# A two-layer diffusion trunk on one core: loading its beginning by single feature tiles, and its last MLP by token tile

## The chip, the cores and the metric

The kernel runs on one core of a Trainium2 chip. The core's engines run beside each other and wait for each other by semaphores: TensorE (PE for its matmuls, PEld for the loads of their stationary operand), VectorE (DVE), ScalarE (ACT), GpSimd (POOL), and SyncE (SP), from whose queue all of this kernel's transfers are issued. Each engine takes its instructions in a fixed order. The metric is the device time of one execution in microseconds (us), lower being better.

## The reference

Two layers over 256 latent tokens and 256 context tokens, model width 1024, all in float32. Cut to what matters here:

```python
for l in range(DEPTH):                                   # DEPTH = 2
    sh1, sc1, g1, sh2, sc2, g2 = ada_mod(c[:, None, :], w_ada[l], b_ada[l])
    u = x * (1.0 + sc1) + sh1                            # the same for the context
    p = split_proj(u @ w_in[l] + b_in[l])                # 76 tiles of 128 columns
    y_a, y_b = local_branches(p, ...)                    # short gated conv | Conformer conv
    y_c = diff_post(diff_latent(q_d, k_d, v_d, ...))     # differential attention
    y_d = na_latent(q_n, k_n, v_n, ...)                  # neighbourhood attention
    y = merge_out(p[I_GATE], (y_a, y_b, y_c, y_d), w_branch[l], b_branch[l], w_o[l])
    x = layer_norm(DEEPNORM_ALPHA * x + g1 * y, ln_g[l, 0], ln_b[l, 0])
    x = layer_norm(DEEPNORM_ALPHA * x + g2 * sq_relu_ffn(x * (1.0 + sc2) + sh2, w_ff1[l], w_ff2[l]),
                   ln_g[l, 1], ln_b[l, 1])
```

`ada_mod` multiplies silu(c) by `w_ada` and gives shifts, scales and gates. In the last layer the context gives only keys and values, so that layer's MLP works on 256 tokens.

## The kernel before, in words

Every product is made of three matmuls: an operand is split into a rounded part and its remainder (for a weight `whi` and `wlo`, for an activation the two tiles of `u`), and `mm3` sums whi x u_hi, whi x u_lo and wlo x u_hi. Weights come in units of 128x1024: a transfer into `raw`, ScalarE makes `whi`, VectorE `wlo`. Units of which both parts are put into two tiles of 512 columns each are called `wh` and `wl`. Activations stand transposed: eight feature tiles k of 128 features, with the 512 tokens (256 latent, 256 context) as columns. A projection unit is eight feature tiles times three matmuls.

Nothing is ordered by hand. Each part of the work is a Python generator with a priority, and `Sched.run` is a list scheduler that has costs of its own for each operation and emits the earliest operation, then the one with the smaller priority number. The order of each engine's instructions comes out of that, and it is fixed in the program.

**The beginning.** The first layer's first modulation (shift and scale) is a product with 8 MB of `w_ada`. `ada_first` does it in four steps j; a step loads eight tiles `a0` (one per 128 rows of the sum, 256 KB each) that give two feature tiles' shift and scale. `ada_first_step` sums them in PSUM (`ada`), copies them (`adrow`), transposes them (`adT`), adds the bias and gives `mod` and `G`. `first_x` loads the input by pairs of feature tiles, latent and context apart (`x0`); `to_u` makes `u` of them. `w_load` puts the first five units' transfers between these (`W_AFTER`), and `first_unit` runs those five products (matrices `M_CA`, `M_CG` of the convolution), each waiting for the pairs of `u`.

**The last layer's MLP input.** `out_proj` multiplies by `w_o` (`wo`), and `residual` and `norm_tile` normalise two token tiles of 128 (tile 0 and tile 1) into `r`. Then `to_u` transposes both tiles by pairs of feature tiles (`uT`), applies scale and shift (`uf`) and splits into `u`. `ff1_rows` runs the first three MLP units k by k over all 256 columns. `LO_AFTER` holds back the remainder `wlo` of the second of these units until tile 1 is normalised.

**The end.** The last product is run for tile 0 and then for tile 1, in two halves of 256 columns. `residual` adds, `norm_tile` waits for the statistics, `normalise` gets 1/sqrt of the variance from GpSimd and applies it with two `stt` (scalar_tensor_tensor) per half row, and `store_out` writes each half.

Of the kernel before, what the change touches and what calls it, by code (L numbers as in the profile page):

```python
# [12 lines left out]
ALU = mybir.AluOpType  # L13
# [12 lines left out]
FIRST = 5  # L26
# [287 lines left out]
class Kernel(Sched):  # L314
# [207 lines left out]
    def constants(self):  # L522
        nc = self.nc
        self.cT = self.const([128, 16], "cTs")
# [31 lines left out]
    def silu_c(self):  # L556
        th = self.const([128, 16], "cth")
        yield self.act(th, self.cT, AF.Tanh, scale=0.5)
        yield self.ts(th, th, 0.5, 0.5, ALU.mult, ALU.add)
        yield self.tt(self.cs[:, :, 0:2], self.cT.re("p (k s) -> p k s", s=2), th.re("p (k s) -> p k s", s=2), ALU.mult)  # L560
        self.signal("cs")
# [5 lines left out]
    def layer_constants(self, l):  # L567
# [3 lines left out]
        if l:  # L571
            yield self.dma(sm, self.SM[l], 128 * NSM * 4)
        else:
            yield self.wait("raw", FIRST - 1)
            yield self.dma(self.rope, self.rope_t.rearrange("c p t -> p c t"), 1 << 18)
# [21 lines left out]
    def w_load(self):  # L597
        for i, (l, name) in enumerate(self.order):
            if i < FIRST:
                yield self.wait("x0", 1, W_AFTER[i])  # L600
# [4 lines left out]
    def w_hi(self):  # L605
        for i in range(len(self.order)):
            yield "prio", 3 if i >= FIRST else FIRST_PRIO
# [5 lines left out]
            else:  # L613
                hi = yield self.alloc("wt", "whi", dt=F32R, name="whi", n=1)
                yield self.act(hi[0], raw, AF.Copy)
            self.signal("whi", i, val=(raw, hi))

    def w_lo(self):
        for i in range(len(self.order)):
            yield "prio", 3 if i >= FIRST else FIRST_PRIO  # L620
# [7 lines left out]
            else:  # L628
                lo = yield self.alloc("wt", "wlo", dt=F32R, name="wlo", n=1)
                yield self.tt(lo[0], raw, hi[0].f, ALU.subtract)  # L630
# [19 lines left out]

    def weight_order(self):
        o = []
        for l in range(DEPTH):
            a = lambda *n: o.append((l, n))
            for ct in range(4):
                a("in", M_CA + ct)
                a("in", M_CG + ct)
# [123 lines left out]
    def ada_first(self):  # L781

        modv = self.modT[0].ap[:, 0:16, :].rearrange("p (c k) s -> p c k s", c=2)
        G = self.const([128, 8, 2], "G00")
        self.aff[0, 0] = G, self.modT[0][:, 0:8, :]
        for j in range(4):
            if j:
                yield self.wait("raw", max(i for i, a in enumerate(W_AFTER) if a < j))
            raws = []
            for k in range(KD):  # L790
                raw = yield self.s("", F32, "a0")
                yield self.dma(raw, self.w_ada0[j, k], 1 << 18)
                raws.append(raw)
            if j == 0:
                yield self.dma(self.sm[0], self.SM[0], 128 * NSM * 4)
            self.signal("a0", j)
            self.spawn(self.ada_first_step(j, raws, modv, G), 6)

    def ada_first_step(self, j, raws, modv, G):
        nc = self.nc  # L800
        yield self.wait("cs")
        ps = yield self.alloc("ps", "ada", name="ada0")
        step = CHUNK if j else 1
        for k0 in range(0, KD, step):
            calls = [(ps.ap[32 * q:32 * q + 32, 0:128], self.cs.ap[:, k, :], raws[k].ap[:, q * 128:q * 128 + 128], k == 0,
                      k == KD - 1, {"tile_position": (0, 32 * q)}) for k in range(k0, k0 + step) for q in range(4)]
            yield self.mm(calls, [ps], [*raws[k0:k0 + step], self.cs], 290 * step)
            self.release(*raws[k0:k0 + step])
# [5 lines left out]
        src = t.ap[:, 0:128].rearrange("p (c k r) -> p c k r", c=2, k=2)[:, :, :, 0:2]  # L814
        out = modv[:, :, 2 * j:2 * j + 2, :]
        b = self.sm[0][:, _SM["ada"]:_SM["ada"] + 16].ap.rearrange("p (c k) -> p c k", c=2)[:, :, 2 * j:2 * j + 2]
        b = b.unsqueeze(3).to_broadcast([128, 2, 2, 2])
        yield self.dve(80, lambda: nc.vector.tensor_tensor(out=out, in0=src, in1=b, op=ALU.add), [self.modT[0]],
                       [t, self.sm[0]])
        self.release(t, row)  # L820
        g = G[:, 2 * j:2 * j + 2, :]
        yield self.ts(g, self.modT[0][:, 8 + 2 * j:10 + 2 * j, :], 1.0, None, ALU.add)
        self.signal("aff", 0, 0, j)
# [52 lines left out]
    def ucut(self, l, j, k, a, b):  # L876

        out = []
        for v in self.u[l, j][k]:
            bufs = v.bufs if a < 256 < b else (v.bufs[0],) if b <= 256 else (v.bufs[1],)  # L880
            out.append(V(v.ap[:, a:b], bufs))
        return out

# [4 lines left out]
    def to_u(self, l, j, s, tiles):  # L888

        yield self.wait("newu", l, j)
        for kp in range(4):
            yield self.wait("aff", l, j, kp)
            G, B = self.aff[l, j]
            if tiles is None:
                t = yield self.wait("x0", s, kp)
            else:
                t = yield self.alloc("ps", "att", name="uT")
                outs, ins = [], []
                for kk in range(2):  # L900
                    for i in range(2):
                        k = 2 * kp + kk
                        o = kk * 256 + i * 128
                        outs.append(t[:, o:o + 128])
                        ins.append(tiles[i][k // 4][:, (k % 4) * 128:(k % 4) * 128 + 128])
                yield self.transposes(outs, ins)
# [14 lines left out]
    def first_x(self):  # L921
        for s in range(2):
            self.spawn(self.to_u(0, 0, s, None), 7)
        for kp in range(4):
            yield self.wait("a0", kp)
            for s in range(2):
                t = yield self.s("", F32, "x0")
                yield self.dma(t, self.x_t[s, kp], 1 << 18)
                self.signal("x0", s, kp, val=t)

    def first_proj(self, ms, n):

        ps = []
        for i, m in enumerate(ms):
            assert self.order[i] == (0, ("in", m))
            self.spawn(self.first_unit(i, n), 40)
        for i, m in enumerate(ms):
            p = yield self.wait("first", i)
            ps.append(p)
        self.w_next = len(ms)  # L940
        self.signal("pace", 0)
# [12 lines left out]

    def first_unit(self, i, n):
        w = yield self.wait("w", i)
        w = Weight(w, 128)
        p = yield self.alloc("ps", "first", name="mm")
        for k in range(KD):
            for s in range(2):  # L960
                yield self.wait("uk", 0, 0, s, k // 2)
            a, b = w(k), self.ucut(0, 0, k, 0, n)
            yield self.mm(self.mm3(p[:, 0:n], a, b, k == 0, k == KD - 1), [p], [*a, *b], 3 * (0.4167 * n + MM))
        self.release(*w.views())
        self.signal("first", i, val=p)
# [485 lines left out]
    def normalise(self, r, stv, ns, gb=None):  # L1451
# [77 lines left out]
    def after_attn_norm(self, l, s, rs):  # L1529

        for i in range(2):
            yield self.wait("z", l, 0, 2 * s + i)
        self.spawn(self.make_x1(l, s, rs), PRIO_X)
# [386 lines left out]
```

## Time and profile before

| | |
|---|---|
| median of 3 runs | 1597.26 us (1596.98 to 1599.57) |
| profiled execution | 1597.91 us, span 1596.0 us |
| TensorE matmuls busy | 1560.8 us (98%), 8688 matmuls |
| weight loads busy | 1336.3 us (84%) |
| VectorE busy | 1306.3 us (82%) |
| ScalarE busy | 870.5 us (55%) |
| read from memory | 250.67 MB |
| mean granted TensorE clock | 0.994 |

The span goes from the first to the last instruction of the profiled execution; its own time has 1.9 us around that. Rows of a profile's timeline are start, length, engine, line, operation, output<-inputs and shape, xN for N instructions in a row; in brackets stands how long the engine had been idle and what ended it. Lengths of pipelined matmuls overlap: the distance of two starts is the rate, the length of one is its latency. Everything of the kernel's helpers is recorded at a few lines (L434 for matmuls, L387, L394 and L414 for VectorE), so tiles tell what a row is.

### The profile page before, as it was taken

What the parts mean: (1) busy time and instruction counts of PE and PEld (TensorE: products, weight loads), DVE (VectorE), ACT (ScalarE), POOL (GpSimd) and SP (SyncE); (2) the same over time, 40 slices, a digit from 0 to 9 for tenths busy, and PEclk for the clock granted to TensorE, in tenths of its full rate; (3) what the DMA queues carried; (4) which work ended last, traced back from release to release, by engine and by line L of the source; (5) the groups of instructions that cost most, each with busy time, mean ns of one, the idle gap of its engine ahead of it and who ended that gap; (6) DMA issues with size and microseconds to landing.
All of it is one profiled execution on the core that took longest, in us unless ns stands there. A gap on an engine that the chain in (4) does not pass through costs nothing.

```text
span 1596.0 us, 23002 instructions
## 1 busy us (share of the span) xinstructions
PE 1560.8 (98%) x8688; PEld 1336.3 (84%) x8688; DVE 1306.3 (82%) x2206; ACT 870.5 (55%) x1411; POOL 12.4 (1%) x51
## 2 busy tenths in 40 slices
PE   6999999999999999999999999999999999989997
PEld 4878888888888788888787878989997999989997
DVE  3999999499999746987687796999999796765566
ACT  3465367454755544742423334766576786476553
POOL 0000000000000000000000000000000000000000
PEclk9999999999999999999999999999999999999999
DMA  9322221455455155456555654533443445645563
GB/s 356 128 73 80 94 91 67 149 181 175 149 176 181 50 171 188 139 186 197 170 192 186 229 185 149 194 127 130 148 140 119 146 158 172 238 146 185 198 223 107
DMA packets 80707, 254.30 MB, mean 159 GB/s; under 512 B 9028, under 2 KB 13892, under 8 KB 80596
## 3 DMA queue, kind: packets, MB, share of 16 engines
q1 hardware_dynamic: 80596, 252.84, 46.7%
q8 instruction: 68, 1.11, 0.3%
q14 instruction: 43, 0.35, 0.1%
HBM read 250.67 MB, written 2.13 MB: 158 GB/s over the span
## 4 chain that ended last, share of the span: by engine, by line
PE 58%; DVE 8%; ACT 1%; issue 1%; POOLq 0%; POOL 0%; DVEq 0%; ACTq 0%
PE mm L434 29%; PE f L434 16%; PE wo L434 4%; PE br L434 4%; DVE wlo L387 2%; DVE conf L414 1%; PE nv L434 1%; PE o L434 1%; PE dv L434 1%; PE PT L494 1%; DVE qk L387 1%; DVE st L1194 1%; PE S L434 0%; DVE pt L387 0%; PE uT L494 0%
## 5 line engine op out<-in xcount | busy, mean ns | idle before, releaser
L434 PE MATMUL mm<-u,whi 128*128 128x512 f32 (+1 forms) x3168 | 786.2, 339 | 0.8 <-ACT u L380 0.3
L434 PEld LDWEIGHTS mm<-u,whi 128*128 128x128 f32 x3168 | 544.8, 190 | 67.9 <-issue 2.8
L434 PE MATMUL mm<-u,wlo 128*128 128x512 f32 (+1 forms) x1584 | 534.1, 337 | 0.6 <-DVE wlo L387 0.6
L387 DVE TENSOR_TENSOR wlo<-raw,whi 128x1024 fp32r<-128x1024 f32 x335 | 408.3, 1220 | 146.7 <-PE mm L434 62.3
L380 ACT ACTIVATE whi<-raw 128x1024 fp32r<-128x1024 f32 x335 | 353.9, 1057 | 320.0 <-DVE wlo L387 115.8
L434 PEld LDWEIGHTS mm<-u,wlo 128*128 128x128 f32 x1584 | 301.1, 190 | 32.6 <-DVE wlo L387 0.8
L434 PE MATMUL f<-whi,a 128*128 128x512 f32 (+1 forms) x760 | 235.3, 388 | 0.0
L414 DVE SCALAR_TENSOR_TENSOR sums<-araw,cs,sums 128x512 f32<-128x512 f32 x280 | 195.2, 745 | 12.5 <-DMA araw<-in_w_ada 12.1
L434 PEld LDWEIGHTS f<-whi,a 128*128 128x128 f32 x760 | 142.3, 188 | 29.7 <-issue 0.8
L434 PE MATMUL f<-wlo,a 128*128 128x512 f32 (+1 forms) x380 | 147.1, 387 | 0.0
L414 DVE SCALAR_TENSOR_TENSOR conf<-glu,sm,conf 128x512 f32<-128x512 f32 (+1 forms) x240 | 137.4, 613 | 0.7
L434 PEld LDWEIGHTS f<-wlo,a 128*128 128x128 f32 x380 | 71.4, 188 | 14.2
L380 ACT ACTIVATE P<-S,st 128x512 f32<-128x512 f32 (+1 forms) x96 | 58.7, 614 | 31.1 <-DVE st L1194 30.7
L434 PE MATMUL wo<-whi,mg 128*128 128x512 f32 (+1 forms) x184 | 56.6, 382 | 0.0
L380 ACT ACTIVATE gth<-mm,hb 128x512 f32<-128x512 f32 (+1 forms) x64 | 36.8, 574 | 34.7 <-PE mm L434 34.5
L1194 DVE TENSOR_REDUCE st<-S 128x1 f32<-128x512 f32 (+1 forms) x96 | 55.1, 589 | 0.3
L434 PE MATMUL S<-qk 128*128 128x512 f32 (+1 forms) x192 | 48.5, 367 | 3.7 <-ACT qk L380 1.2
L380 ACT ACTIVATE qk<-ra 64x512 fp32r<-64x512 f32 (+1 forms) x67 | 37.7, 563 | 22.7 <-DVE ra L387 21.4
L380 ACT ACTIVATE bh<-br,hb 128x512 f32<-128x512 f32 (+1 forms) x64 | 36.3, 573 | 20.8 <-PE br L434 20.6
L380 ACT ACTIVATE a2f<-mm 128x512 f32<-128x512 f32 (+1 forms) x64 | 30.7, 481 | 30.5 <-PE mm L434 30.5
L387 DVE TENSOR_TENSOR a<-a2f,a 128x512 fp32r<-128x512 f32 (+1 forms) x64 | 35.4, 554 | 11.4 <-ACT a L380 11.4
L434 PE MATMUL dv<-whi,u 128*128 128x512 f32 x128 | 43.3, 398 | 0.5 <-ACT P L380 0.5
(206 smaller groups left out, 1907.2 us busy)
## 6 DMA issues: line engine op xcount, KB each, us to landing
raw<-in_W SPq DMA_DIRECT2D x344, 512.0 KB
araw<-in_w_ada SPq DMA_DIRECT2D x80, 512.0 KB
a<-in_w_ada SPq DMA_DIRECT2D x32, 256.0 KB
bt<-in_rpb SPq DMA_DIRECT2D x32, 128.0 KB
row<-g SPq DMA_DIRECT2D x12, 256.0 KB
x<-in_x_t SPq DMA_DIRECT2D x8, 256.0 KB
row<-in_ln_g SPq DMA_DIRECT2D x8, 256.0 KB
row<-in_ln_b SPq DMA_DIRECT2D x8, 256.0 KB
```

Of the source, the lines that this page charges most:

```text
L380: lambda: nc.scalar.activation(out=out.ap, in_=in_.ap, func=func, **kw),
L387: return self._op(eng, cost, lambda: e.tensor_tensor(out=out.ap, in0=x.ap, in1=y.ap, op=op), [out], [x, y])
L414: return self._op("DVE", cost, lambda: nc.vector.scalar_tensor_tensor(out=out.ap, in0=x.ap, scalar=a(s), in1=y.ap, op0=op0, op1=op1), [out ...
L434: nc.tensor.matmul(out=out, lhsT=x, rhs=y, start=start, stop=stop, **kw)
L494: nc.tensor.transpose(o.ap, i.ap, ident.ap)
L1194: yield self.dve(68 + 1.04 * nk, lambda: nc.vector.tensor_reduce(out=mx.ap, in_=S.ap, axis=AX.X, op=ALU.max, negate=True), [mx], [S])
```

## The change

It has four parts.

1. The beginning goes by single feature tiles. `load_all` issues for each k four modulation tiles (each now two of the eight rows of the sum, for one feature tile's shift and scale), the input's tile (latent and context together), and one transfer `W0[k]` with the k-th rows of six units (128x768). `ada_first` is run for each k; its sums of even and odd rows stand apart and are added after the transpose. `first_u` makes `u` of one k, 512 columns wide, and `first_proj` runs six units' products for that k into six PSUM banks. The biases of the modulation come with `cT`.
2. In the last layer `to_u_tile` makes the MLP's input for one token tile as soon as that tile is normalised, and `ff1_rows` runs tile 0's products for all k (128 columns each) and then tile 1's. The first MLP unit is among those that are kept in tiles of 512 columns.
3. In the last normalisation tile 0's `norm_tile` gets priority 40 instead of 1.
4. `normalise` emits the first `stt` of both halves ahead of the second ones.

```diff
+    def load_all(self):
+        for k in range(KD):
+            raws = []
+            for i in range(4):
+                raw = yield self.s("", F32, "a0")
+                yield self.dma(raw, self.w_ada0[k, i], 1 << 18)
+                raws.append(raw)
+            self.spawn(self.ada_first(k, raws), 6)
+            t = yield self.s("", F32, "x0")
+            yield self.dma(t, self.x_t[k], 1 << 18)
+            self.signal("x0", k, val=t)
+            raw = yield self.alloc("wt", "raw", name="raw")
+            yield self.dma(raw[:, 0:FIRST * 128], self.W0[k], FIRST * 128 * 512)
+            self.signal("raw", k, val=raw)
...
     def ada_first(self, j, raws):
         yield self.wait("cs")
         ps = yield self.alloc("ps", "ada", name="ada0")
+        for i, raw in enumerate(raws):
+            yield self.mm([(ps.ap[32 * q:32 * q + 32, 0:128], self.cs.ap[:, 2 * i + q // 2, :],
+                            raw.ap[:, q * 128:q * 128 + 128], i == 0, i == 3, {"tile_position": (0, 32 * q)})
+                           for q in range(4)], [ps], [raw, self.cs], 290)
+            self.release(raw)
...
     def first_proj(self, ms, n):
+        for m in ms:
+            p = yield self.alloc("ps", "first", name="mm")
+            ps.append(p)
+        for k in range(KD):
+            hi, lo = yield self.wait("w", k)
+            yield self.wait("u0", k)
+            b = self.ucut(0, 0, k, 0, n)
+            for i, p in enumerate(ps):
+                a = hi[0][:, i * 128:i * 128 + 128], lo[0][:, i * 128:i * 128 + 128]
+                yield self.mm(self.mm3(p[:, 0:n], a, b, k == 0, k == KD - 1), [p], [*a, *b], 3 * (0.4167 * n + MM))
...
+    def to_u_tile(self, l, j, i, tile):
+        yield self.wait("newu", l, j)
+        for h in range(2):
+            t = yield self.alloc("ps", "att", name="uT")
+            yield self.transposes([t[:, q * 128:q * 128 + 128] for q in range(4)],
+                                  [tile[h][:, q * 128:q * 128 + 128] for q in range(4)])
+            f = yield self.s("tmp", F32, "uf")
+            for q in range(4):
+                k = 4 * h + q
...
+                c = slice(q * 128, q * 128 + 128)
+                yield self.affine_any(f[:, c], t[:, c], G[:, k, 0:1], B[:, k, 0:1])
+                yield from self.split(f[:, c], *self.ucut(l, j, k, i * 128, i * 128 + 128))
+                self.signal("uk", l, j, i, k)
...
     def normalise(self, r, stv, ns, gb=None):
             for c, h in enumerate(r):
                 yield self.stt(h, h, mv[:, 0:1], g[c], ALU.subtract, ALU.mult)
+            for c, h in enumerate(r):
                 yield self.stt(h, h, rs, b[c], ALU.mult, ALU.add)
                 self.signal("out", c, h.bufs[0])
...
     def after_attn_norm(self, l, s, rs):
+        if self.by_tile(l, 1):
+            for i in range(2):
+                yield self.wait("z", l, 0, i)
+                self.spawn(self.to_u_tile(l, 1, i, rs[i]), 2)
...
     def ff1_rows(self, l, ms, n):
-        for k in range(KD):
-            yield self.wait("uk", l, 1, 0, k // 2)
-            for p, w in zip(ps, ws):
-                a, b = w(k), self.ucut(l, 1, k, 0, n)
-                yield self.mm(self.mm3(p[:, 0:n], a, b, k == 0, k == KD - 1), [p], [*a, *b], 3 * (0.4167 * n + MM))
+        for i in range(n // 128):
+            for k in range(KD):
+                yield self.wait("uk", l, 1, i, k)
+                for p, w in zip(ps, ws):
+                    a, b = w(k), self.ucut(l, 1, k, i * 128, i * 128 + 128)
+                    yield self.mm(self.mm3(p[:, i * 128:i * 128 + 128], a, b, k == 0, k == KD - 1), [p], [*a, *b],
+                                  3 * (0.4167 * 128 + MM))
...
-                self.spawn(self.norm_tile(l, 1, t, yacc[t], sts[t]), 1)
+                self.spawn(self.norm_tile(l, 1, t, yacc[t], sts[t]), 40 if l == DEPTH - 1 and t == 0 else 1)
...
-                          if l == DEPTH - 1 and (n[:2] == ("wo", 1) and n[2] < 2 or n[:3] == ("f2", 3, 1) and n[3] < 2)}
+                          if l == DEPTH - 1 and (n == ("f1", 0) or n[:2] == ("wo", 1) and n[2] < 2 or n[:3] == ("f2", 3, 1) and n[3] < 2)}
```

Three places show what this does to the order. The first is TensorE (PE) in the beginning, where products (`mm`) and sums of the modulation (`ada`, one row for a tile `a`) follow each other. Before:

```order
L434 MATMUL mm<-u,wl 128x512
L434 MATMUL ada_328<-a_218,cs 32x128 x4
L434 MATMUL ada_328<-a_220,cs 32x128 x4
L434 MATMUL ada_328<-a_222,cs 32x128 x4
L434 MATMUL ada_328<-a_229,cs 32x128 x4
L434 MATMUL mm<-u,wh 128x512 x2
L434 MATMUL mm<-u,wl 128x512
L434 MATMUL mm<-u,wh 128x512 x2
```

And now, at a similar place (the fifth feature tile's modulation among the third's and fourth's products):

```order
L431 MATMUL mm<-u,wlo 128x512
L431 MATMUL ada_379<-a_221,cs 32x128 x4
L431 MATMUL mm<-u,whi 128x512 x2
L431 MATMUL mm<-u,wlo 128x512
L431 MATMUL ada_379<-a_223,cs 32x128 x4
L431 MATMUL mm<-u,whi 128x512 x2
L431 MATMUL mm<-u,wlo 128x512
L431 MATMUL ada_379<-a_225,cs 32x128 x4
L431 MATMUL mm<-u,whi 128x512 x2
L431 MATMUL mm<-u,wlo 128x512
L431 MATMUL ada_379<-a_227,cs 32x128 x4
```

Four tiles that stood together stand singly between products: behind the first product there are 19 such switches for 26 tiles, where there were five for 24.

The second place is the last layer's MLP input. On PE, from the last `wo` of tile 1; each feature tile's transpose is one `uT`. Before:

```order
L434 MATMUL wo<-whi,mg 128x256
L494 MATMUL uT<-ident,r 128x128 x8
L434 MATMUL mm<-u,whi 128x256 x2
L434 MATMUL mm<-u,wlo 128x256
L434 MATMUL mm<-u,whi 128x256 x2
```

And now, where the twelve transposes are tile 0's eight and the first four of tile 1:

```order
L431 MATMUL wo<-whi,mg 128x256
L491 MATMUL uT<-ident,r 128x128 x12
L431 MATMUL mm<-u,wh 128x128 x2
L431 MATMUL mm<-u,wl 128x128
L431 MATMUL mm<-u,whi 128x128 x2
L431 MATMUL mm<-u,wlo 128x128
```

The products have half the columns and twice the number, and tile 1's first transposes stand ahead of all of them. On VectorE (DVE) at the same place, from tile 1's last residual (`r<-wo`) to the two remainders `wlo` that wait for tile 1's normalisation (`r<-r,st`). Before:

```order
L387 TENSOR_TENSOR r<-wo,row 128x256
L414 SCALAR_TENSOR_TENSOR r<-x_13348,r 128x256
L1492 BN_STATS st<-r 128x6
L1456 BN_AGGR st<-st 128x2
L394 TENSOR_SCALAR st<-st 128x1 x2
L394 TENSOR_SCALAR r<-r,st 128x512
L387 TENSOR_TENSOR wlo<-raw,whi 128x1024 x2
```

And now:

```order
L384 TENSOR_TENSOR r<-wo,row 128x256
L391 TENSOR_SCALAR uf<-uT,G_13581,B_13582 128x128
L411 SCALAR_TENSOR_TENSOR r<-x_13352,r 128x256
L1524 BN_STATS st<-r 128x6
L384 TENSOR_TENSOR u<-uf,u 128x128
L1487 BN_AGGR st<-st 128x2
L391 TENSOR_SCALAR uf<-uT,G_13581,B_13582 128x128
L391 TENSOR_SCALAR st<-st 128x1
L384 TENSOR_TENSOR u<-uf,u 128x128
L391 TENSOR_SCALAR uf<-uT,G_13581,B_13582 128x128
L391 TENSOR_SCALAR st<-st 128x1
L391 TENSOR_SCALAR r<-r,st 128x512
```

Tile 0's affines and differences stand between the steps of tile 1's normalisation; two more of them follow, then a `wlo`, another difference and the second `wlo`.

The third place is DVE at the end, from the last addition of the product (`yf`). Before:

```order
L387 TENSOR_TENSOR yf<-f_15737,row 128x256
L414 SCALAR_TENSOR_TENSOR yacc<-yacc,st,row 128x512
L387 TENSOR_TENSOR yacc<-yf,yacc 128x256
L1492 BN_STATS st<-yacc 128x6
L1456 BN_AGGR st<-st 128x2
L394 TENSOR_SCALAR st<-st 128x1
L414 SCALAR_TENSOR_TENSOR yacc<-yacc,st,row 128x512 x4
```

And now:

```order
L384 TENSOR_TENSOR yf<-f_15837,row 128x256
L384 TENSOR_TENSOR yacc<-yf,yacc 128x256
L1524 BN_STATS st<-yacc 128x6
L1487 BN_AGGR st<-st 128x2
L391 TENSOR_SCALAR st<-st 128x1
L411 SCALAR_TENSOR_TENSOR yacc<-yacc,st,row 128x512 x5
```

Tile 0's step has gone from the middle of tile 1's chain to its end.

More of the change, by code (lines that the diff above doesn't have):

```diff
@@ L573, in layer_constants @@
         else:
-            yield self.wait("raw", FIRST - 1)
+            yield self.wait("raw", KD - 1)
             yield self.dma(self.rope, self.rope_t.rearrange("c p t -> p c t"), 1 << 18)
@@ L594, in layer_constants @@
         self.signal("const", l)
[L597 to L600, printed above, removed]
+    def load_all(self):
[12 more added lines that the diff above has]
+            self.signal("raw", k, val=raw)
+            if not k:
+                yield self.dma(self.sm[0], self.SM[0], 128 * NSM * 4)
+        for i, (l, name) in enumerate(self.order[KD:], KD):
             raw = yield self.alloc("wt", "raw", name="raw")
@@ L629, in w_lo @@
                 lo = yield self.alloc("wt", "wlo", dt=F32R, name="wlo", n=1)
[L630 removed]
+                n = self.width(i)
+                yield self.tt(lo[0][:, 0:n], raw[:, 0:n], hi[0][:, 0:n].f, ALU.subtract)
             self.release(raw)
@@ L649, in blocks, with conv_tiles @@
         return [(0, (0, 1)), (1, (0,)), (1, (1,))]
+    @staticmethod
+    def conv_tiles():
+        return [m + ct for ct in range(4) for m in (M_CA, M_CG)]
     def weight_order(self):
@@ L654, in weight_order @@
             a = lambda *n: o.append((l, n))
-            for ct in range(4):
-                a("in", M_CA + ct)
-                a("in", M_CG + ct)
+            first = FIRST if not l else 0
+            if first:
+                for k in range(KD):
+                    a("first", k)
+            for m in Kernel.conv_tiles()[first:]:
+                a("in", m)
             def diff(st):
@@ L779, in rows4, with ada_first @@
         return b.unsqueeze(1).to_broadcast([4, 32, b.shape[1]])
[L781 to L789, printed above, removed]
-            for k in range(KD):
[L791 to L799, printed above, removed]
+    def ada_first(self, j, raws):
         nc = self.nc
+        G, mod = self.aff[0, 0][0], self.modT[0]
         yield self.wait("cs")
         ps = yield self.alloc("ps", "ada", name="ada0")
[L803 to L808, printed above, removed]
+        for i, raw in enumerate(raws):
[3 more added lines that the diff above has]
+            self.release(raw)
         row = yield self.s("", F32, "adrow")
@@ L894, in to_u @@
             G, B = self.aff[l, j]
[L895 to L906, printed above, removed]
+            t = yield self.alloc("ps", "att", name="uT")
+            outs, ins = [], []
+            for kk in range(2):
+                for i in range(2):
+                    k = 2 * kp + kk
+                    o = kk * 256 + i * 128
+                    outs.append(t[:, o:o + 128])
+                    ins.append(tiles[i][k // 4][:, (k % 4) * 128:(k % 4) * 128 + 128])
+            yield self.transposes(outs, ins)
             for kk in range(2):
@@ L1529, in after_attn_norm @@
     def after_attn_norm(self, l, s, rs):
-        for i in range(2):
-            yield self.wait("z", l, 0, 2 * s + i)
-        self.spawn(self.make_x1(l, s, rs), PRIO_X)
-        yield from self.to_u(l, 1, s, rs)
+        if self.by_tile(l, 1):
+            for i in range(2):
+                yield self.wait("z", l, 0, i)
+                self.spawn(self.to_u_tile(l, 1, i, rs[i]), 2)
+            self.spawn(self.make_x1(l, s, rs), PRIO_X)
+            for i in range(2):
+                yield self.wait("ut", l, 1, i)
+        else:
+            for i in range(2):
+                yield self.wait("z", l, 0, 2 * s + i)
+            self.spawn(self.make_x1(l, s, rs), PRIO_X)
+            yield from self.to_u(l, 1, s, rs)
         self.signal("used", l, s)
@@ L1719, in main @@
                 self.spawn(self.layer_constants(1), 70)
-                first = yield from self.first_proj([M_CA, M_CG, M_CA + 1, M_CG + 1, M_CA + 2, M_CG + 2][:FIRST], n)
+                first = yield from self.first_proj(self.conv_tiles()[:FIRST], n)
             for ct in range(4):
@@ L1862, in _layout @@
         put("lnb", f["ln_b"][l].reshape(16, 128).T)
-        put("ada", f["b_ada"][l, 0:2048].reshape(16, 128).T)
     cT = np.stack([f["c"].reshape(8, 128), f["c_ctx"].reshape(8, 128)], -1).transpose(1, 0, 2).reshape(128, 16)
+    cT = np.concatenate([cT, f["b_ada"][0, 0:2048].reshape(16, 128).T], 1)
     p = np.arange(128)
```

113 lines of the change are left out of this document (57 added, 56 removed).

## The prediction

> **What bounds the kernel now.** I read the page's totals first, then busy time by stretch, then the PE rows around its few idle stretches.
>
> ```profile
> span 1596.0 us, 23002 instructions
> PE 1560.8 (98%) x8688; PEld 1336.3 (84%) x8688; DVE 1306.3 (82%) x2206; ACT 870.5 (55%) x1411; POOL 12.4 (1%) x51
> ...
> 10.00:38.00 28.00, 20.89 (x223) 13.72 (x220) 12.17 (x35) 13.16 (x31) 0.00 (x0) 1.00 1.05 400
> ...
> 280.00:320.00 40.00, 40.00 (x182) 33.28 (x181) 19.86 (x29) 18.02 (x24) 0.00 (x0) 1.00 0.48 156
> ...
> 1320.00:1360.00 40.00, 40.00 (x336) 40.00 (x335) 25.91 (x40) 24.03 (x38) 0.00 (x0) 1.00 0.57 184
> ...
> 1398.30:1400.80 2.50, 0.10 (x1) 0.00 (x0) 1.69 (x5) 0.90 (x1) 0.50 (x1) 0.99 0.57 187
> 1400.80:1407.50 6.70, 5.62 (x23) 4.93 (x24) 4.55 (x8) 4.41 (x9) 0.05 (x1) 0.50 0.26 87
> ...
> 1416.20:1587.20 171.00, 170.97 (x1102) 156.64 (x1102) 108.07 (x134) 99.28 (x160) 0.55 (x1) 1.00 0.55 188
> 1587.20:1596.00 8.80, 0.00 (x0) 0.00 (x0) 5.32 (x11) 0.00 (x0) 0.92 (x1) 0.77 0.31 119
> ```
>
> The stretches show length, then busy time and count of PE, PEld, DVE, ACT and POOL, then the granted clock, the DMA share and GB/s. PE is busy 98%, so only its idle stretches and its own work can move the end: the beginning (DMA near its limit, 400 GB/s), the gap at 1398 before the last layer's MLP, and the 8.8 us after the last matmul. In layer 1 a 256-column matmul takes 40/336 = 0.119 us, and the weight loads beside them (PEld) are busy all of the time too.
>
> **The beginning.** A "unit" is 24 matmuls of 512 columns. I count to the end of the sixth unit.
>
> ```profile
> 7.34 0.20 PEld L434 LDWEIGHTS ada<-a,cs 128*32 128x32 f32 x8 [0.45 <-DMA a<-in_w_ada]
> ...
> 10.18 0.20 PEld L434 LDWEIGHTS ada<-a,cs 128*32 128x32 f32 x8 [0.44 <-DMA a<-in_w_ada]
> ...
> 13.09 0.76 DVE L387 TENSOR_TENSOR u<-uf,u 128x256 fp32r<-128x256 f32 x2 [0.52 <-ACT u L380]
> ...
> 14.91 1.22 PE L434 MATMUL mm<-u,wh 128*128 128x512 f32 x2 [3.21 <-ACT wh L380]
> 15.94 0.63 PE L434 MATMUL mm<-u,wl 128*128 128x512 f32 x1
> 16.36 1.34 PE L434 MATMUL mm<-u,wh 128*128 128x512 f32 x2
> ...
> 18.06 2.06 PE L434 MATMUL ada<-a,cs 128*32 128x128 f32 x64
> 20.53 0.33 PE L494 MATMUL adT<-ident,adrow 128*128 128x128 f32 x1 [0.41 <-ACT adrow L380]
> ...
> 25.98 0.40 PE L434 MATMUL mm<-u,wl 128*128 128x512 f32 x1
> 26.31 1.08 PE L434 MATMUL ada<-a,cs 128*32 128x128 f32 x32
> 27.32 0.73 PE L434 MATMUL mm<-u,wh 128*128 128x512 f32 x2
> 27.89 0.39 PE L434 MATMUL mm<-u,wl 128*128 128x512 f32 x1
> ...
> 55.97 0.61 PE L434 MATMUL mm<-u,whi 128*128 128x512 f32 x2
> ...
> 61.41 0.61 PE L434 MATMUL mm<-u,whi 128*128 128x512 f32 x2
> ```
>
> Before, the first product starts at 14.91, and unit six runs from 55.97 to 61.41: 5.44 us, 0.227 a matmul. New, modulation, input and weights come by feature tile, 1.70 MB each, and at 400 GB/s one lands every 4.3 us. PE needs more than that for a tile, so PE is the bound. The steps:
> - Start. The first input tile needs four modulation tiles (matmul at 7.34) instead of eight (10.18). Before, the first pair of `u` follows the eighth by 3.3 us (13.45). New, two 256-column affines and a weight split stand in the chain; I estimate 1.1 us more, so about 11.7, with the first matmul just ahead: 11.3.
> - 144 matmuls x 0.227 = 32.7.
> - 26 modulation tiles still come behind that start. 64 records against 32 (2.06 and 1.08 us) give 0.245 a tile: 6.4.
> - Every switch between products and modulation drains PE. From 25.98 to 27.89 are 1.91 us: three matmuls (0.68), four tiles (0.98), so 0.25 for the switch. The old order switches five times, the new one 19 times (single tiles, mostly) behind the start: 19 x 0.25 = 4.8. This is the term that eats the earlier start.
> - Seven small transposes at 0.12 (0.8), and the slow clock: matmuls 0.42 apart (15.94 to 16.36) until 18.06, 3.2 us of half rate. From 11.3 it lasts as long or up to twice: loss 1.6 to 3.2, I take 2.4.
> - Waits: the second tile's transpose has only some 2.6 us of products behind it where its chain takes 3.4, and the sixth stands right behind its own sums (0.41 in the row at 20.53): 1.2, between 0 and 2.
>
> Sum 11.3 + 32.7 + 6.4 + 4.8 + 0.8 + 2.4 + 1.2 = 59.6, a gain of 1.8. If switches and waits cost nothing and the clock rises early: 52.8, a gain of 8.6; with the first input 0.9 later and the clock and waits at their worst 62.1, a loss of 0.7. I stay at 1.8, since the switch has a row of its own. Next late: the convolutions. All six units end together, so VectorE's taps begin some 8 us later. Its slack at 280:320 (20 of 40 us idle) covers them; without that cover they would cost up to 8. Layer 0's attention is reordered by this; I put 0 on it. SP issues as many descriptors as it did, and its waits for a `raw` buffer lie some 9 us ahead of the data.
>
> **The last layer's MLP input.**
>
> ```profile
> 1398.01 0.28 PE L434 MATMUL wo<-whi,mg 128*128 128x256 f32 x1
> ...
> 1401.61 1.75 PE L494 MATMUL uT<-ident,r 128*128 128x128 f32 x7 [3.21 <-DVE r L394]
> ...
> 1407.37 0.70 PE L494 MATMUL uT<-ident,r 128*128 128x128 f32 x4
> 1407.82 0.48 PE L434 MATMUL mm<-u,whi 128*128 128x256 f32 x2
> ...
> 1416.19 0.39 PE L434 MATMUL mm<-u,wlo 128*128 128x256 f32 x1 [0.63 <-DVE wlo L387]
> ```
>
> ```profile
> 1398.33 0.42 DVE L387 TENSOR_TENSOR r<-wo,row 128x256 f32<-128x256 f32 x1 [1.08 <-PE wo L434]
> 1398.79 0.42 DVE L414 SCALAR_TENSOR_TENSOR r<-x,r 128x256 f32<-128x256 f32 x1
> ...
> 1401.02 0.54 DVE L394 TENSOR_SCALAR r<-r,st 128x512 f32<-128x512 f32 x1
> 1401.47 2.35 DVE L387 TENSOR_TENSOR wlo<-raw,whi 128x1024 fp32r<-128x1024 f32 x2
> ```
>
> ```profile
> L434 PEld LDWEIGHTS mm<-u,whi 128*128 128x128 f32 x3168 | 544.8, 190 | 67.9 <-issue 2.8 <-DVE u L387 2.0 <-ACT a2f L380 0.8
> ...
> L434 PEld LDWEIGHTS ada<-a,cs 128*32 128x32 f32 x256 | 6.7, 119 | 10.8 <-DMA a<-in_w_ada 4.9 <-DVE cs L387 3.9 <-issue 1.1
> ```
>
> Before, PE waits 3.2 us for tile 1's normalisation, runs at half clock to 1407.5, and the fourth MLP unit's third matmul starts at 1416.19, so that unit ends at 1416.19 + 22 x 0.119 = 1418.8. New, three things:
> - The first four transposes of tile 1 stand ahead of tile 0's products in PE's queue, so the products still wait for tile 1. And on VectorE three affines and two differences of tile 0 are put between tile 1's residual and its normalisation (0.3 to 0.4 us each; 0.7 of them in the wait for POOL): tile 1 is normalised some 0.8 later (0.3 to 1.3), at 1401.9 instead of 1401.02.
> - The two `wlo` that follow have three small operations ahead or between: the second is done at about 1405.4 instead of 1403.8. The first nine products need both, so 135 of 144 remain then.
> - Each product has half the columns, but as many weight loads per product: 144 instead of 72. The trace has no such 128-column product. By streaming alone (0.119 for 256 columns, 0.227 for 512, so 0.42 ns a column) it would be 0.067. By the weight load it isn't: 190 ns for 128 columns and 119 for 32 make 0.74 ns a column, 95 ns for 128, and loads that start 0.119 apart are back to back in the row of 1320:1360. Ends 0.067 and 0.119; I take 0.115, nearest to the row in which PEld is full.
>
> The Trainium skill, "TensorE: Matmul & The Clock Gate", section "LDWEIGHTS (loading the stationary operand)", puts a weight load at its columns over 1.2, which makes 107 ns here and 1.1 us less in this sum; the 0.74 ns a column agree roughly.
>
> So 1405.4 + 135 x 0.115 (15.5) + four transposes (0.45) + half clock for some 4 us more (2.0) + the fourth unit 2.9 = 1426.3 against 1418.8: +7.5 (with 0.107 and an early clock +5.4, with 0.119 and a late one +8.9). The split of the first MLP weight into 512-column halves costs 0.1 on ACT and VectorE, which idle there.
>
> **The end.**
>
> ```profile
> 1586.89 0.28 PE L434 MATMUL f<-whi,a 128*128 128x256 f32 x1
> ...
> 1587.45 0.42 DVE L387 TENSOR_TENSOR yf<-f,row 128x256 f32<-128x256 f32 x1
> 1587.78 0.74 DVE L414 SCALAR_TENSOR_TENSOR yacc<-yacc,st,row 128x512 f32<-128x512 f32 x1
> 1588.44 0.42 DVE L387 TENSOR_TENSOR yacc<-yf,yacc 128x256 f32<-128x256 f32 x1
> ...
> 1589.72 0.74 DVE L414 SCALAR_TENSOR_TENSOR yacc<-yacc,st,row 128x512 f32<-128x512 f32 x1
> 1590.90 2.20 DVE L414 SCALAR_TENSOR_TENSOR yacc<-yacc,st,row 128x512 f32<-128x512 f32 x3 [0.44 <-POOL st L1458]
> ```
>
> Tile 0's step at 1587.78 moves behind tile 1's statistics and so do two steps of tile 1: five in a row, 3.3 us from about 1589.4, so 1592.7 instead of 1593.1. Gain 0.4, between 0 and 1.1.
>
> **Sum.** -1.8 + 7.5 - 0.4 = +5.3 on the profiled execution's 1597.91 (span 1596.0, 1.9 around it): 1603.2. The median of the runs lies 0.65 lower, so I say 1602.6.
>
> **Rivals.**
> - The weight load hides (not slower): 128-column products at 0.067. Then the middle is 1405.4 + 9.0 + 0.45 + 1.5 + 2.9 = 1419.3, +0.5, and the whole -1.7: 1595.6. For it: nothing shows a load that binds alone; against: the full PEld row. It decides below about 0.080, where the middle's loss equals the other gains. Chance 0.17. The same page, section "Back-to-back issue gap", has about 81 ns for sustained 128-column matmuls, which would make the whole +0.2.
> - Switches cost little, since a single tile's loads might slip in beside a product: beginning -8.6, whole -1.5: 1595.8. The row at 26.31, 0.33 behind the matmul ahead, speaks against. Chance 0.13.
> - Both: 1588.8, chance 0.04.
> - Layer 0's new order, or a later half clock stretch: 2 to 4 more, 1604.6 to 1606.6, chance 0.08.
>
> **Numbers.** The forecast has 0.58; with its own terms at their ends it reaches from 1599.5 to 1605.7. The range goes to the first two rivals and the last: 1594.5 to 1606.5. About 0.2% (3.2 us) is what a measurement can tell: slower than 1600.5 has 0.61, faster than 1594.1 has 0.13, between 0.26.
>
> **What would show it.** The sixth unit's end (forecast 59.6) and the gaps at each switch; products of 128 columns 0.11 to 0.12 apart with PEld full; the first of them only behind tile 1's transposes; the second `wlo` at 1405 on the old time scale; five steps in a row at the end. I am wrong if those products are 0.07 apart, or the sixth unit ends by 54.

## The result and the profile after

The changed kernel takes 1618.02 us (median of four runs, 1616.82 to 1621.89) against 1598.08 us (1596.98 to 1599.57) for the kernel before: 1.0124 times as long, 95% interval 1.0112 to 1.0137. It is slower, as predicted, but by 20 us and not by 5. The profiled execution took 1617.44 us (span 1615.5), 19.5 more than the one of before.

The page's totals of the changed kernel:

```profile
span 1615.5 us, 23177 instructions
PE 1586.0 (98%) x8764; PEld 1355.6 (84%) x8764; DVE 1308.6 (81%) x2223; ACT 875.5 (54%) x1418; POOL 12.2 (1%) x51
```

PE has 76 matmuls more (8764 against 8688), and 25 us more of busy time: it did not wait for longer, its matmuls took longer. Busy time by stretch around the MLP's start tells where (length, then busy time and count of PE, PEld, DVE, ACT and POOL, then the granted clock, DMA share and GB/s):

```profile
1396.98:1400.40 3.42, 0.39 (x4) 0.15 (x2) 3.06 (x12) 1.62 (x4) 0.55 (x1) 1.00 0.85 286
1400.40:1437.90 37.50, 37.04 (x174) 37.04 (x175) 15.13 (x35) 11.27 (x28) 0.00 (x0) 0.50 0.12 39
1437.90:1441.30 3.40, 3.40 (x30) 3.40 (x29) 2.50 (x4) 2.44 (x6) 0.00 (x0) 1.00 0.57 201
1441.30:1606.90 165.60, 165.60 (x1060) 151.27 (x1058) 102.52 (x126) 93.64 (x147) 0.55 (x1) 1.00 0.54 182
1606.90:1615.50 8.60, 0.00 (x0) 0.00 (x0) 5.40 (x11) 0.00 (x0) 0.92 (x1) 0.80 0.33 123
```

The second row is the finding: PE is busy for 37.0 of 37.5 us, and yet the granted clock stays at 0.50 all of that time. Before, the stretch at half clock lasted 6.8 us (the row at 1400.80 in the prediction). PE's timeline there, cut to its turning points:

```profile
1396.65 0.28 PE L431 MATMUL wo<-whi,mg 128*128 128x256 f32 x1
1396.77 0.60 PE L491 MATMUL uT<-ident,r 128*128 128x128 f32 x4
1400.86 1.97 PE L491 MATMUL uT<-ident,r 128*128 128x128 f32 x8 [3.49 <-DVE r L391]
1402.48 0.67 PE L431 MATMUL mm<-u,wh 128*128 128x128 f32 x2
1402.95 0.41 PE L431 MATMUL mm<-u,wl 128*128 128x128 f32 x1
1403.16 0.63 PE L431 MATMUL mm<-u,whi 128*128 128x128 f32 x2
...
1434.01 0.73 PE L431 MATMUL mm<-u,whi 128*128 128x256 f32 x2
...
1438.66 0.40 PE L431 MATMUL mm<-u,whi 128*128 128x256 f32 x2
```

From 1402.48 on, three 128-column products start every 0.64 us: 0.213 each. The 256-column products begin at 1434.01, and 3.9 us later the clock is back. The matmul at the fourth unit's end (1438.66) stands in the trace of before at 1418.93:

```profile
1418.93 0.40 PE L434 MATMUL mm<-u,whi 128*128 128x256 f32 x2
```

It is 19.7 us late, and everything behind it stays 19.7 us late up to the last matmul.

The parts of the 19.5 us: up to the last `wo` the changed kernel is 1.36 us ahead (1396.65 against 1398.01), from there to the fourth unit's end it loses 21.1, and the time behind the last matmul is 0.2 shorter (8.60 us against 8.83).

### The profile page after: what moved, and what is told of

Read it like the earlier page. It is cut to its first block, busy times and chain, and to the rows that moved or that the text cites. A ratio compares the mean times of both kernels' runs of the same rounds, so it can differ in the third digit from the quotient of the medians.

```text
span 1615.5 us, 23177 instructions
## 1 busy us (share of the span) xinstructions
PE 1586.0 (98%) x8764; PEld 1355.6 (84%) x8764; DVE 1308.6 (81%) x2223; ACT 875.5 (54%) x1418; POOL 12.2 (1%) x51
## 4 chain that ended last, share of the span: by engine, by line
PE 87%; DVE 8%; ACT 2%; issue 1%; DMA 1%; SPq 0%; DVEq 0%; ACTq 0%
PE mm L431 49%; PE f L431 16%; PE br L431 8%; PE wo L431 4%; PE nv L431 2%; PE o L431 2%; DVE wlo L384 2%; PE S L431 2%; PE dv L431 2%; PE PT L491 1%; PE ada L431 1%; DVE conf L411 1%; DVE qk L384 1%; DVE st L1225 1%; DVE ra L384 0%
## 5 line engine op out<-in xcount | busy, mean ns | idle before, releaser
L431 PE MATMUL mm<-u,whi 128*128 128x512 f32 (+2 forms) x3264 | 824.5, 343 | 0.8 <-DVE u L384 0.5
L431 PEld LDWEIGHTS mm<-u,whi 128*128 128x128 f32 x3264 | 568.5, 193 | 71.4 <-issue 5.1
L431 PE MATMUL mm<-u,wlo 128*128 128x512 f32 (+2 forms) x1632 | 556.7, 341 | 0.3 <-DVE st L391 0.3
L377 ACT ACTIVATE whi<-raw 128x1024 fp32r<-128x1024 f32 (+1 forms) x341 | 358.5, 1052 | 345.0 <-DVE wlo L384 125.6
L384 DVE TENSOR_TENSOR wlo<-raw,whi 128x1024 fp32r<-128x1024 f32 (+1 forms) x341 | 413.9, 1214 | 152.4 <-PE mm L431 67.7
L431 PEld LDWEIGHTS mm<-u,wlo 128*128 128x128 f32 x1632 | 315.0, 193 | 33.9 <-DVE wlo L384 0.5
L377 ACT ACTIVATE a2f<-mm 128x512 f32<-128x512 f32 (+1 forms) x64 | 30.7, 482 | 33.9 <-PE mm L431 33.9
L431 PEld LDWEIGHTS S<-qk 128*128 128x128 f32 x192 | 32.0, 189 | 14.7 <-ACT qk L377 4.8
L384 DVE TENSOR_TENSOR a<-a2f,a 128x512 fp32r<-128x512 f32 (+1 forms) x64 | 35.4, 556 | 10.9 <-ACT a L377 10.8
```

Source lines behind the costliest of these rows:

```text
L377: lambda: nc.scalar.activation(out=out.ap, in_=in_.ap, func=func, **kw),
L384: return self._op(eng, cost, lambda: e.tensor_tensor(out=out.ap, in0=x.ap, in1=y.ap, op=op), [out], [x, y])
L431: nc.tensor.matmul(out=out, lhsT=x, rhs=y, start=start, stop=stop, **kw)
```

## The experiments

Two theories stood at first. "Share": the short products themselves keep the clock down. "Gap": the long half clock follows from the wait in front of them, whatever their width. A third, "count" (the number of columns that the products stream decides), came out of the first four runs. The granted clock of these traces changes in steps of 3.41 us: the stretches at half clock below last 6.83, 10.24, 30.72 and 37.5 us, which are two, three, nine and eleven of them. All runs shared a chip with runs of the kernel before, whose medians were 1599.0, 1598.6 and 1599.4 us.

**Without the MLP part** (`no_tiles`).

```diff
     def by_tile(l, j):
-        return l == DEPTH - 1 and j == 1
+        return False
```

and `ff1_rows` and the set of kept weights as before.

> The new beginning and the new end, with the last layer's MLP input and first MLP products as before. In the trace of the changed kernel the last layer's output product ends 1.36 us earlier than before, and the time behind the last matmul is 0.2 us shorter. Theory 'share' (the whole loss is the stretch at half clock, which the 128-column products themselves keep up) and its rival 'gap' (the long half clock comes from the longer wait in front of them) both give 1598.1 - 1.4 - 0.2 = 1596.5, between 1595.5 and 1597.5, with a half clock of two steps (6.8 us) at the MLP as before. Above 1600 would mean that the beginning carries part of the loss.

Measured 1597.68 us (median of 11), ratio to before 0.9994, interval 0.9985 to 1.0003. The half clock at the MLP lasts two steps, as before:

```profile
1402.60:1409.43 6.83, 6.55 (x28) 5.86 (x28) 3.83 (x6) 3.94 (x9) 0.00 (x0) 0.50 0.24 77
```

The whole loss is in the MLP part. By the interval the new beginning and end are worth something between a loss of 0.5 us and a gain of 2.4; the median lies 0.2 above the range of this forecast.

**Products of 256 columns** (`wide_products`).

```diff
-        for i in range(n // 128):
-            for k in range(KD):
-                yield self.wait("uk", l, 1, i, k)
+        for k in range(KD):
+            for i in range(n // 128):
+                yield self.wait("uk", l, 1, i, k)
...
-                    a, b = w(k), self.ucut(l, 1, k, i * 128, i * 128 + 128)
+                a, b = w(k), self.ucut(l, 1, k, 0, n)
```

> The changed kernel, with the token tiles' input still made one by one and the same transposes ahead of the products, but the first three MLP units run over 256 columns, each feature tile as soon as both token tiles have it. 'Share': the clock is back at full after two or three steps of 3.41 us, the loss of the MLP part shrinks from 21 to at most 6 us: 1597 to 1603. 'Gap': the wait in front is the same 3.5 us, so the half clock again lasts some 37 us, of which about 18 us are lost: 1612 to 1619.

Measured 1597.99 us, 0.9994 (0.9985 to 1.0003). The stretch at half clock:

```profile
1400.34:1410.58 10.24, 8.29 (x36) 7.60 (x37) 8.39 (x23) 4.72 (x13) 0.00 (x0) 0.50 0.15 54
```

Three steps instead of eleven, with the same wait of 3.49 us in front of the transposes. That speaks against "gap": the width of the products decides how long the clock stays low.

**The wait filled** (`filled_gap`): in `to_u_tile`, ahead of tile 1's first transposes,

```diff
+            if i and not h:
+                hi, _ = yield self.wait("w", self.order.index((l, ("f1", 0))))
+                for _ in range(16):
+                    yield self.mm([(t.ap, hi[0].ap[:, 0:128], hi[0].ap, True, True, {})], [t], [hi[0]], 227)
```

> The changed kernel, with 16 matmuls of 512 columns, whose result is overwritten, in PE's wait of 3.5 us in front of tile 1's transposes (3.6 us at full clock), so that PE isn't idle there. 'Gap': the clock never falls, the 144 products run 0.107 us apart, and the time is 1618.0 less half of 37.5 us, 1599 (1598 to 1602). 'Share': the clock falls one or two steps after the 128-column products begin, and comes back only behind them; the time falls by 0 to 4 us, 1614 to 1618.

Measured: six of nine executions at 1613.5 to 1615.9 us, three at 1601.0 to 1604.1 (not five and four, as a later expectation says; median 1613.65, ratio 1.0071, 1.0047 to 1.0095). One of the first kind was profiled:

```profile
1398.85:1402.26 3.41, 3.36 (x23) 2.77 (x22) 3.12 (x9) 2.59 (x7) 0.55 (x1) 1.00 0.26 105
1402.26:1405.67 3.41, 2.62 (x24) 2.48 (x23) 3.41 (x11) 1.47 (x5) 0.00 (x0) 1.00 0.35 125
1405.67:1436.39 30.72, 30.72 (x147) 30.72 (x147) 9.39 (x20) 7.39 (x18) 0.00 (x0) 0.50 0.11 38
```

Neither theory said this. The clock was at full when the 128-column products began, and fell one step later, after a step with 0.79 us of idle time (a wait for a `wlo`) and, counted by their starts, 22 products with 2,816 columns; in the three shorter executions it didn't fall (their mean granted clock is 0.998 to 0.999, that of the others 0.989 to 0.990).

**Short products in a busy stretch** (`steady`), on `no_tiles`: in `proj`, for MLP units 10 to 15 all matmuls in pieces of 128 columns, for units 18 to 23 two of three, for 26 to 31 one of three.

```diff
+        if short == 3:
+            parts = [(0, 128), (128, 256)]
+        elif short:
...
+                three = [(x[0], y[0], 256), (x[0], y[1], 128 if short > 1 else 256), (x[1], y[0], 128)]
```

> The kernel with the MLP as before (as in the first of these runs), but in the middle of the last layer's MLP, where PE has been busy for 30 us and more, six units in a row run as 128-column products (all three matmuls of a product), six later ones with two of three matmuls in 128 columns, and six more with one of three. By 0.107 us for a 128-column and 0.119 for a 256-column matmul at full clock, a unit takes 5.1, 4.4 and 3.6 us instead of 2.9. 'Gap': the clock stays at full in all of them, +13.6 + 9.1 + 4.6 = +27 on the first of these runs, 1624. 'Share': an array that streams 0.053 of 0.107 us counts as too little; the first six fall to half clock after one or two steps and take 50 to 60 us instead of 17; streamed shares of 0.50, 0.58 and 0.71 would show where the bound is; with only the first below it 1645 to 1655, with the first two 1670 to 1680.

Measured 1628.46 us, 1.0186 (1.0172 to 1.0200). The three stretches:

```profile
1458.20:1490.32 32.12, 32.12 (x290) 32.11 (x288) 9.48 (x11) 12.78 (x23) 0.00 (x0) 1.00 0.30 102
...
1518.02:1545.11 27.09, 27.09 (x242) 27.09 (x241) 10.25 (x13) 11.91 (x21) 0.00 (x0) 1.00 0.48 151
1572.76:1594.44 21.68, 21.68 (x190) 21.68 (x189) 11.82 (x16) 11.92 (x21) 0.00 (x0) 1.00 0.44 146
```

All of them at full clock: 288 products of 128 columns in 32.1 us, 0.1115 each. So the same products that can't raise the clock from half keep it once it is at full; "share" in its first form falls as well. What fits all four runs is "count": the clock of the next step of 3.41 us follows from the columns streamed in this one, and at half clock the same products stream half as many. 128 columns every 0.213 us make 2,050 a step, which left the clock at half, and every 0.1115 us 3,920, which kept it at full; 256 every 0.213 us make 4,100, which raised it. The bound lies between.

**Smaller products in a busy stretch** (`small_steady`), on `no_tiles`:

```diff
+            pieces = ([(0, 64), (64, 128), (128, 192), (192, 256)], [(0, 88), (88, 172), (172, 256)])[name[1] // 8 - 1]
+        for a, b in pieces or parts or [(0, n)]:
```

> The MLP input as before, and in the middle of the last layer's MLP six units in a row with every product cut into pieces of 64 columns, and six later ones with pieces of 88, 84 and 84. PE has work all of the time there. Theory 'count': the clock of the next step of 3.41 us hangs on the columns that PE streamed in this one, in whatever state the clock is; in the traces so far it stayed or rose above about 2,900 and fell or stayed low below about 2,700. At 0.11 us a product the 64-column pieces make 2,000 a step, so the clock falls within two steps without any idle time and stays low: 576 products x 0.215 = 124 us less 3, against 17 for whole units, +104. The pieces of 85 make 2,640, just below the bound: low as well 90 us against 17 (+73), kept at full 47 (+30). 1598 + 104 + 30 to 73 = 1732 to 1775. Rival 'idle': the clock falls only where PE has idle time, so it stays at full throughout: +46 + 30, 1674.

Measured 1773.26 us, 1.1094 (1.1078 to 1.1109), where "idle" gave 1674. The steps at the fall and the stretch behind it, for 64 columns and for 85:

```profile
1457.90:1461.31 3.41, 3.41 (x33) 3.41 (x32) 0.24 (x1) 1.06 (x1) 0.00 (x0) 1.00 0.49 160
1461.31:1574.72 113.41, 113.41 (x534) 113.41 (x534) 8.25 (x10) 10.83 (x20) 0.00 (x0) 0.50 0.07 24
...
1608.09:1611.50 3.41, 3.41 (x33) 3.41 (x32) 0.00 (x0) 0.00 (x0) 0.00 (x0) 1.00 0.15 54
1611.50:1692.04 80.54, 80.54 (x380) 80.54 (x379) 8.26 (x10) 10.83 (x20) 0.00 (x0) 0.50 0.16 53
```

PE was never idle, and the clock fell after one whole step of such products (31 x 64 = 1,984 and 31 x 84 = 2,604 columns; the 2,800 of a later expectation is too high) and stayed low: a clock can be lost with no gap at all.

**More filling** (`filled_more`): `range(22)` for `range(16)`.

> The changed kernel with 22 instead of 16 filling matmuls in PE's wait, so that the remainders wlo are there when the first products reach them, and no wait of 0.8 us stands among the 128-column products. 'Count': with 16, the step at 1402.3 had that wait and 2,750 columns and the clock fell in five of nine executions; without the wait a step has 3,900, so it stays at full in all of them: the 1601 to 1604 of the other four, 1600 to 1604, with no half clock at the MLP. 'Idle in front' (the clock falls from whatever precedes the 128-column products, and now and then not): again executions at 1601 and at 1614 in a mixture.

Measured 1601.48 us, all nine executions between 1600.95 and 1604.09, ratio 1.0019 (1.0010 to 1.0029).

```profile
1402.90:1420.00 17.10, 17.10 (x156) 17.10 (x155) 10.90 (x28) 6.60 (x17) 0.00 (x0) 1.00 0.10 32
```

The wait among the products is gone, and with it the mixture. Compared with the changed kernel 16.5 us come back, and nothing was done but to keep the clock.

**Where the bound is** (`bound`), on `wide_products`: at the MLP's start one matmul of three in two pieces; in units 10 to 15 pieces of 99 columns on average.

```diff
+                calls = [(p.ap[:, 0:n], hi.ap, uh.ap, k == 0, False, {}), (p.ap[:, 0:128], lo.ap, uh.ap[:, 0:128], False, False, {}),
+                         (p.ap[:, 128:n], lo.ap, uh.ap[:, 128:n], False, False, {}), (p.ap[:, 0:n], hi.ap, ul.ap, False, k == KD - 1, {})]
...
+            two, three = [(0, 128), (128, 256)], [(0, 88), (88, 172), (172, 256)]
+                ops = [(x[0], y[0], two), (x[0], y[1], three), (x[1], y[0], three)]
```

> The kernel with 256-column products at the start of the MLP, but one matmul of three cut into two of 128 there (192 columns on average), so that at half clock (0.213 us each) a step of 3.41 us has 3,070 columns; and six units in the middle of the MLP with pieces of 99 columns on average, which make 3,030 a step at full clock (0.1115 each), where pieces of 85 with 2,800 fell. Theory 'count' with one bound for both states, at about 2,850: the clock rises in the MLP's start within four steps, and stays at full in the middle: 1598 + 3 to 5 for 24 more products at the start and + 24 for the middle (372 products, 41 us instead of 17): 1625 to 1628. Rival 'two bounds' (it falls below about 2,850, but rises only far above, say 3,500): all 96 products of the start run at half clock, 1631 to 1636. If 3,030 is already too little at full clock, the middle takes 80 us: 1660 and more.

Measured 1660.85 us, 1.0381 (1.0364 to 1.0398). The last step at half clock in the MLP's start and the one behind it; then the step in the middle after which the clock fell, and what followed:

```profile
1408.48:1411.90 3.42, 3.42 (x17) 3.42 (x18) 1.91 (x5) 0.51 (x2) 0.00 (x0) 0.50 0.00 1
1411.90:1415.30 3.40, 3.40 (x31) 3.40 (x32) 1.23 (x4) 1.31 (x4) 0.00 (x0) 1.00 0.00 0
1463.10:1466.51 3.41, 3.41 (x33) 3.41 (x32) 0.37 (x1) 1.06 (x1) 0.00 (x0) 1.00 0.48 154
1466.51:1537.10 70.59, 70.59 (x334) 70.59 (x333) 8.25 (x10) 10.83 (x20) 0.00 (x0) 0.50 0.12 38
```

So my bound of 2,850 was too low and the middle went the third way that the expectation names. One bound between 2,944 and 3,072 columns a step would serve both states here; "two bounds" isn't needed, though one kernel's two steps don't exclude it. A step of `filled_gap` shows how sharp the count is: at half clock from 1429.60 it has seven 128-column and then nine 256-column products, 3,200 columns by their starts, and the clock rose only one step later. If the count is taken one or two matmuls earlier (0.2 to 0.4 us), that step has 3,072 or 2,944. So the bound is known to some 250 columns, and one bound for both states is a fit, not shown.

**A better version.** `filled_before_mlp` is `no_tiles` with 14 such matmuls in front of the transposes in `to_u`:

```diff
+            if l == DEPTH - 1 and j == 1 and not kp:
+                hi, _ = yield self.wait("w", self.order.index((l, ("f1", 0))))
+                for _ in range(14):
+                    yield self.mm([(t.ap, hi[0].ap[:, 0:128], hi[0].ap[:, 0:512], True, True, {})], [t], [hi[0]], 227)
```

> The new beginning and end with the MLP as before, and 14 matmuls of 512 columns, whose result is overwritten, in PE's wait of 3.2 us in front of the MLP input's transposes (14 x 0.227 = 3.2). 'Count': the clock stays at full, and two steps at half clock (6.8 us), in which PE did 3.6 us of work less the wait's own end, are saved: 1597.7 - 2.5 = 1595.2, between 1594 and 1596.5. 'Idle': the same. Without an effect, 1597.7.

Measured 1595.24 us, 0.9979 (0.9970 to 0.9988). The clock stays at full through the wait and behind it:

```profile
1395.70:1399.10 3.40, 3.40 (x18) 2.67 (x16) 2.25 (x7) 1.47 (x3) 0.55 (x1) 1.00 0.46 154
1399.10:1402.50 3.40, 2.16 (x15) 1.56 (x14) 3.12 (x5) 3.06 (x7) 0.00 (x0) 1.00 0.34 93
```

"Count" forecast this, but its bound doesn't give it: the step from 1398.81 has only 2,048 columns by their starts, half of them in eight transposes, and by "count" the clock should have fallen behind it. `warm_start` adds 14 matmuls at the beginning too:

```diff
+        for _ in range(14):
+            yield self.mm([(ps[0].ap[:, 0:128], self.ident.ap, self.ident.ap, True, True, {})], [ps[0]], [self.ident], 430)
```

> As the one before, and 14 matmuls of the unit matrix with itself among the first modulation tiles, so that PE has less idle time before the first product. 'Count': the clock is at full from about 8 us on instead of 14.6, and the 3.1 us of products at half clock are done in half the time: 1.5 us less, if the matmuls of full float32 count for the clock as the others do: 1593.7, between 1592 and 1596. 'Late': they hold up the modulation that the first input waits for, and nothing is won: 1595 to 1597.

Measured 1593.63 us, 0.9969 (0.9958 to 0.9979): faster than both kernels, with the half clock at the MLP gone. Its first rows on PE:

```profile
1.36 2.93 PE L431 MATMUL mm<-ident 128*128 128x128 f32 x12 [1.36 <-POOL ident masks.py:199]
...
12.51 0.50 PE L431 MATMUL mm<-u,whi 128*128 128x512 f32 x1
13.32 0.50 PE L431 MATMUL mm<-u,whi 128*128 128x512 f32 x1 [0.30 <-DVE u L384]
```

The clock is at full from 10.9 us (14.6 in the changed kernel, some 8 by the expectation of "count"). But the first products come later too (12.51 and 13.32 instead of 11.49), so "late" is half right, and the 1.6 us between the two medians is near what the runs can tell.

## Why the prediction was wrong, step by step

**The beginning: the sum met the trace, its terms less so.** Forecast for the end of the sixth unit was 59.6, the trace has 59.38 (the 144 products start at 11.49, and the next one at 59.38):

```profile
11.49 1.22 PE L431 MATMUL mm<-u,whi 128*128 128x512 f32 x2
...
28.34 0.40 PE L431 MATMUL mm<-u,wlo 128*128 128x512 f32 x1
28.67 0.43 PE L431 MATMUL ada<-a,cs 128*32 128x128 f32 x8
29.03 0.72 PE L431 MATMUL mm<-u,whi 128*128 128x512 f32 x2
29.59 0.40 PE L431 MATMUL mm<-u,wlo 128*128 128x512 f32 x1
...
49.34 0.40 PE L431 MATMUL mm<-u,wlo 128*128 128x512 f32 x1
49.67 0.65 PE L431 MATMUL ada<-a,cs 128*32 128x128 f32 x16
50.24 0.73 PE L431 MATMUL mm<-u,whi 128*128 128x512 f32 x2
50.82 0.39 PE L431 MATMUL mm<-u,wlo 128*128 128x512 f32 x1
...
59.38 0.61 PE L431 MATMUL mm<-u,whi 128*128 128x512 f32 x2
```

Three products take 0.68 us. With a single modulation tile among them they take 1.25 (28.34 to 29.59), with two together 1.48 (49.34 to 50.82): 0.23 a tile and 0.34 a switch, where the prediction has 0.245 and 0.25. So the 19 switches cost 6.5 us and not 4.8, and the 26 tiles 6.0 and not 6.4. Of the 47.9 us from 11.49 to 59.38, products (32.7), tiles, switches and transposes (0.8) make 46.0. That leaves 1.9 for the slow clock and the waits, where the prediction has 3.6. The errors cancelled: that the sum came out so near is luck in part. The rival "switches cost little" falls all the same.

The gain of 2.03 us at that point has shrunk to 1.36 at the last `wo`. The late convolutions were covered, as said: the first `br` products that read the two convolutions' results (`ya`, `yb`) start 2.4 and 2.1 us ahead (219.61 against 222.04, 447.72 against 449.83). Layer 0's new order wasn't free in its parts. The stretch at half clock around 540 was absent from the profiled execution, and the gain stood at 4.4 us at layer 0's first `wo` (606.20 against 610.58). Some 3.0 of it were given back later; the times from one start to the next of the 80 sums `ada<-sums,ones` grew from 9.5 to 12.2 us. That these two nearly cancelled, so that the sum came out near the 0 that I had put, is luck as well.

**The MLP input: the terms near, but for one.** On VectorE:

```profile
1400.27 0.54 DVE L391 TENSOR_SCALAR r<-r,st 128x512 f32<-128x512 f32 x1
...
1402.58 1.21 DVE L384 TENSOR_TENSOR wlo<-raw,whi 128x1024 fp32r<-128x1024 f32 x1
```

Tile 1's normalisation starts at 1400.27, which is 1401.6 on the old time scale (forecast 1401.9), and the second `wlo` ends at 1403.79, or 1405.15 (forecast 1405.4). A 128-column product takes 0.1115 us at full clock (`steady`) where I took 0.115; the rival with 0.067 falls. The page "TensorE: Matmul & The Clock Gate" of the Trainium skill, section "LDWEIGHTS (loading the stationary operand)", puts a weight load at its columns over 1.2, by which 128 columns take 107 ns (an estimate): the 0.1115 us at full clock are near it, and the 0.213 at half clock are twice as much.

The step that failed is the term "half clock for some 4 us more (2.0)". The half clock lasted 37.5 us instead of 6.8, 30.7 us more, in which half of the time is lost: 15.4. With 15.4 in the place of 2.0 the middle's +7.5 becomes +20.9, and 21.1 were measured. I had carried over from before that the clock comes back after two steps, though in that row 256-column products run, and had not asked what a step of 128-column products would stream: at half clock both start 0.213 us apart, so a step has half the columns. That the clock depends on this at all is what the prediction lacked. The rival "a later half clock stretch" named the right resource, at 2 to 4 us.

The same page of the Trainium skill, section "What's actually happening", has the full clock come back after about 3.4 us of sustained activity, and calls it a budget of time, not of a number of matmuls. By that the half clock would have ended within 7 us of the first product at 1402.48 (an estimate, two such times). The traces here differ: it didn't end for 31 us of 128-column products, with PE busy throughout, and with 64 columns it set in without a gap.

**The end was right.** The five steps are one row, and end at 1612.43, 5.5 us behind the last matmul (5.9 before): the forecast 0.4, of which 0.2 show in the span.

```profile
1609.04 3.39 DVE L411 SCALAR_TENSOR_TENSOR yacc<-yacc,st,row 128x512 f32<-128x512 f32 x5
```

Open is whether the clock counts columns, or the time that the array streams with one bound for each state: with only two clocks these runs can't tell the two apart. The rule isn't complete either where transposes stand among the matmuls. In layer 0's attention steps with 2,304 (`steady`, from 534.78) and 2,816 columns (the changed kernel, from 533.39) kept the full clock, and so did the step of 2,048 in `filled_before_mlp`; one of 2,048 in `warm_start` (from 533.17) lost it. If each transpose is counted twice, these four have 3,328, 3,328, 3,072 and 3,072 columns, which fits a bound near 3,072. That was fitted afterwards, and no run tests it.

## What to carry to other kernels

Before cutting matmuls into shorter ones behind a wait, work out the columns streamed in a step of 3.41 us at half clock, not at full: here 2,050 (128 columns every 0.213 us) kept TensorE at half speed for as long as they lasted, while 3,072 brought it back. A row of PE that is busy all of the time says nothing of its speed; read the granted clock beside it. Where a wait in front of a busy stretch can't be removed, matmuls whose result is thrown away can keep the clock through it: they gave about 0.15% with the MLP as before, and 1% in the changed kernel.

## What was unexpected of the hardware

The clock has two stable states for one and the same stream of instructions: 128-column products ran at 0.1115 us for 32 us and at 0.213 us for 31 us, by the state that they met. Pieces of 64, 85 and 99 columns (on average) lost the clock with PE busy all of the time, after a step with 2,944 columns or fewer. With a wait of 0.79 us among the 128-column products (in the profiled execution of `filled_gap`) the same kernel took 1601 to 1604 us in three executions and 1613 to 1616 in six; with that wait gone it took 1601 to 1604 in all nine.
